# Longer estimated delays in the planner that lays down TensorE's order (RWKV scan of a hybrid attention layer)

## The chip, the cores and the metric

The kernel runs on one core of one Trainium2 chip. The time is the device time of one execution in microseconds (us); lower is better. Before the change three runs took 3445.99 us in the median (3438.13 to 3447.74).

## The reference

One layer for two groups of tokens, 512 "sample" and 128 "prompt" tokens of width 2048, in float32. An adaLN modulation is followed by one input projection. Its columns feed latent attention (8 heads) and a bidirectional RWKV-7 time mixing (16 heads of 64), whose state S is updated token by token in both directions. Then come one output projection, a post-norm, a SwiGLU feed-forward network and a second post-norm.

```python
def _wkv_scan(s0, r, decay, k, v, kk, a, reverse):
    def step(S, inp):
        r_t, w_t, k_t, v_t, kk_t, a_t = inp
        sa = jnp.einsum("bhvk,bhk->bhv", S, -kk_t)
        S = S * w_t[:, :, None, :] + sa[..., None] * (kk_t * a_t)[:, :, None, :] + v_t[..., None] * k_t[:, :, None, :]
        return S, jnp.einsum("bhvk,bhk->bhv", S, r_t)
...
        logw = -jax.nn.softplus(-(w0 + jnp.tanh(wd) @ w_up).astype(F32)) - 0.5
        decay = jnp.exp(-jnp.exp(logw))
        a = jax.nn.sigmoid(a0 + ad @ a_up)
```

## The kernel before

Features lie on the 128 partitions and the 640 tokens along the free axis, in two halves of 320. Every large product is made from a high and a low part of each operand (`whi`, `wlo` of a weight, `xh`, `xl` of an activation), so one 128-column weight tile against one 128-row activation tile is three pairs of matmuls, one for each half.

The program has three stages in time. **Stage 1** computes the input projection (job `main`), the modulation vectors (`first_mods`, `wmods`) and, as soon as their columns are there, the RWKV scan (job `rwkv`). **Stage 2** begins when `main` has ended: attention takes the place of the projection beside what is left of the scan. **Stage 3** is the output projection and the feed-forward network; its order is not touched by the edited tables.

The scan is done in chunks of 64 tokens instead of token by token. It runs over 8 pairs of heads, and for each pair over two halves j = 0, 1: 16 **units**, one after another, each dependent on the last. A unit is a chain of small products on TensorE with work on VectorE (DVE), ScalarE (ACT) and GpSimd (POOL) between them:

- `rwkv_load` (once a pair): load r, k, v from DRAM, square k, a product with a block matrix (`m<-cst,kk`), a power on POOL, a product that spreads the result (`m<-cst,rt`);
- `rwkv_decays`: the low-rank products for decay and gate, one group for each direction (`m<-xw,lw`, `m<-xa,lw`, `m<-xl,lw`); for every unit but the first they are laid down by a side job, beside the chain of the unit ahead;
- `rwkv_prep`: operands `nk` and `pr` on DVE, ACT and POOL; then `rwkv_grams`: Gram products in three batches (`m<-pr,nk`), each evacuated by two ACT copies (to `mab`, `mrb`) and a DVE product;
- `inverse`: a long piece on DVE that ends in the tile `tc`, then four rounds of products (`m<-tc,mab`, `m<-pm,uc`, `m<-t,mab`, `m<-u,pm`);
- `rwkv_chain`: five state updates, each of three products: `m<-sv,pr` (evacuated to `xs`), `m<-xs,uf` (evacuated to `zv` by one ACT copy and one DVE copy), `m<-zv,bk` (to the next state `sv`); `outputs` adds the products of the step before.
- `rwkv_post` (once a pair, in a side job beside the next pair's first unit): group norm and the gate product `m<-sg,gw`, then a store of `y` to DRAM.

TensorE (PE) executes its instructions in order, and this order is written out by a small planner at build time, not by the framework. Each job is a generator; after it has issued a group of matmuls it yields an estimated delay in us. The planner keeps one clock, `T.now`, which advances by an estimate of each matmul's length. At each step it takes, of the jobs whose delay is over, the one with the lowest rank: the scan first (0), its side jobs, the modulation (2), attention (3), the projection (4).

```python
        now = max(self.pe.now, min(j.ready for j in free))
        job = min((j for j in free if j.ready <= now), key=lambda j: j.rank)
...
            job.ready = w if isinstance(w, Job) else self.pe.now + w
```

So a delay says how much work of the other jobs stands in PE's queue between a product of the scan and the next product that depends on it. The projection and attention are the filler. The delays are in two tables, `HOPS[0]` for stage 1 and `HOPS[1]` for stage 2. The planner has no say at run time: where a delay is too short, PE reaches the dependent product early and waits there, with the filler queued behind it. The orders on DVE, ACT and POOL, and on the queue SP that issues the DMAs, are made by the framework's own scheduler; they follow from PE's order.

Of the kernel before, what the change touches and what calls it, by code (L numbers as in the profile page):

```python
# [46 lines left out]
for _n, _w in (("ident", 128), ("gmask", 128), ("lmask", 32), ("par", 2), ("blk", 128), ("cen", 128), ("blk2", 2), ("sel", 2),  # L47
# [12 lines left out]
TURN = 0.5  # L60
W_HOP = 2.4
M_HOP = 4.9
RANK_R = 0
RANK_S = 1
RANK_W = 2
# [1 line left out]
RANK_Q = 3  # L67
RANK_M = 4

HOPS = ({"load": 3.73, "pow": 3.84, "kk": 1.18, "dec": 0.92, "prep": 1.68, "vr": 2.17, "tv": 0.36, "bk": 0.36, "gram": 0.75,  # L70
         "inv": 12.0, "d32": 1.2, "d32b": 1.92, "d64": 1.44, "d64b": 1.44, "x": 0.48, "s": 0.72, "p": 0.72,
         "bon0": 0.92, "bon": 0.36, "cen0": 0.0, "cen": 0.36, "ysq": 0.28, "pow2": 3.84, "gup0": 0.0, "gup": 0.36,
         "wm": 5.98, "ev": 1.0, "sq": 3.77},
        {"load": 3.69, "pow": 2.76, "kk": 0.42, "dec": 0.36, "prep": 3.6, "vr": 1.2, "tv": 0.85, "bk": 0.54, "gram": 0.79,
         "inv": 14.0, "d32": 1.51, "d32b": 1.96, "d64": 1.3, "d64b": 1.44, "x": 0.61, "s": 0.72, "p": 0.72,
         "bon0": 0.94, "bon": 0.36, "cen0": 0.0, "cen": 0.51, "ysq": 0.71, "pow2": 3.84, "gup0": 0.0, "gup": 0.36,
         "rms": 2.33, "krs": 7.15, "rope": 0.6, "sc": 0.0, "turn": 0.0, "val": 0.0})
N_WS = 2
# [81 lines left out]
def step_kernel(ctx: ExitStack, tc: tile.TileContext, a: dict, o: dict, upto: int = 99, npairs: int = NPAIR, dbg=None):  # L160
    nc = tc.nc
    HOP = dict(HOPS[0])
    V, A, G, DMA = nc.vector, nc.scalar, nc.gpsimd, nc.sync
# [21 lines left out]
    def rtile(name, n, tag, bufs, dtype=F32):  # L185
        return rp.tile([P, n], dtype, tag=tag, name=nm(name), bufs=bufs)

    def slot(name, dtype=F32):
        return rtile(name, NT, "s", N_S, dtype)
# [7 lines left out]
    def half5(name):  # L197
        return rtile(name, 512, "h5", 4)
# [18 lines left out]
    def vcol(name, i=0, n=1):  # L217
        return vec[:, VEC[name][0] + i: VEC[name][0] + i + n]

    def con(name):  # L220
        return cst[:, CST[name][0]: CST[name][0] + CST[name][1]]
# [5 lines left out]
    def tt(eng, out, x, y, op):  # L227
        eng.tensor_tensor(out=out, in0=x, in1=y, op=op)  # L228
# [7 lines left out]
    def stt(out, x, s, y, op0, op1):  # L236
        V.scalar_tensor_tensor(out=out, in0=x, scalar=s, in1=y, op0=op0, op1=op1)

    def act(out, x, f, bias=0.0, scale=1.0):
        A.activation(out, x, f, bias=bias, scale=scale)  # L240
# [15 lines left out]
    def load_raw(src):  # L256
        raw = tile_("raw", 512, "raw", N_RAW)[:, :src.shape[-1]]
        DMA.dma_start(out=raw, in_=src)
        return raw
# [211 lines left out]
    def first_tiles():  # L471
        fs = (0, *range(2, 2 + N_PART), 1)
        ws = Weights(a["w_in"][f, k0 // 4][:, k0 % 4 * P: (k0 % 4 + nk) * P] for k0, nk in GROUPS for f in fs)
        for k0, nk in GROUPS:
            last = k0 + nk == KT
            while len(h1) < k0 + nk:
                yield 1.0
            yield M_HOP
            for f in fs:
# [56 lines left out]
    def rows(h):  # L536
        return slice(64 * h, 64 * h + 64)

    def ch(t):
        return t.rearrange("p (c t) -> p c t", t=C)  # L540
# [8 lines left out]
    def wide(name):  # L549

        return rtile(name, 2 * NT, "w", N_W).rearrange("p (c b t) -> p c b t", b=2, t=C)

    def h10(t):
        return t.rearrange("p (c t) -> p c t", t=32)
# [3 lines left out]
    for t in nd_bufs + u_bufs:  # L558
        G.memset(t, 0.0)

    def inverse(mab):

# [10 lines left out]
        x = half5("ix")  # L575
# [27 lines left out]
        tc_ = half5("tc")  # L603
        V.transpose(tc_[:, :HN], uc[:, :HN])
        u, t = h10(uc[:, :HN]), h10(tc_[:, :HN])
        yield HOP["inv"]
        blocks = [(e, b) for e in range(NCH) for b in range(4)]

        def d32(lhs, rhs):
# [14 lines left out]
        u, t = h10(u2[:, :HN]), h10(t2[:, :HN])  # L624
# [24 lines left out]
    def stat_cols(sq, rhs, n, bank=mps):  # L649

        ps = bank()
        for c in range(5):
            T.matmul(ps[:, c * n: c * n + n], sq[:, c * P: c * P + P], rhs, start=True, stop=True)
        return ps

    def spread(st, n, ps2=None):

        outs = []
        w_ = P // n
        for q, (c0, w) in enumerate(SPL):  # L660
            ps = mps() if ps2 is None else ps2[:, q, :]
            for j in range(w // P):
                c = c0 // P + j
                for e in range(n):
                    lhs = st[:, c * n + e: c * n + e + 1].broadcast_to([P, w_])
                    T.matmul(ps[w_ * e: w_ * e + w_, j * P: j * P + P], lhs, ident, start=True, stop=True)
            outs.append(ps)
        return outs

    def rpow(src, n, eps, scale, floor=False):  # L670
        st = small("st")
        if floor:
            ts(V, st[:, :n], src, eps, None, ALU.max)
        else:
            ts(V, st[:, :n], src, scale, eps)
        rt = small("rt")
        tt(G, rt[:, :n], st[:, :n], mhalf[:, :n], ALU.pow)
        return rt

    def nat(d, j):  # L680

        h = j if d == 0 else 1 - j
        return slice(h * HN, h * HN + HN)
# [5 lines left out]
    def rwkv_load(i):  # L689
        sh = {"carry": rtile("cy", 2 * C, "cy", 1)}  # L690
        raw = load_raw(a["lora"][i])

        lw = sh["lw"] = rtile("lw", 512, "lw", 1, F32R)
        A.copy(lw, raw)
        for r_, c_ in ((slice(64, 128), slice(0, 256)), (slice(0, 64), slice(256, 512))):
            tt(V, lw[r_, c_], raw[r_, c_], lw[r_, c_].bitcast(F32), ALU.subtract)
        for j, n in enumerate("rkv"):
            sh[n] = slot(n)
            DMA.dma_start(out=sh[n], in_=rkv_d[i][j])
        k = sh["k"]  # L700
        kk = sh["kk"] = slot("kk")
        act(kk, k, AF.Square, scale=vcol("kk", i))
        yield HOP["load"]
        ss = stat_cols(kk, con("blk2"), 2)
        rn = rpow(ss[:, :10], 10, 1e-24, 0, floor=True)
        yield HOP["pow"]
        for (c0, w), ps in zip(SPL, spread(rn, 2)):
            stt(kk[:, c0: c0 + w], k[:, c0: c0 + w], vcol("kk", i), ps[:, :w], ALU.mult, ALU.mult)
        sh["ks"] = slot("ks")
        yield HOP["kk"]  # L710
        return sh
# [43 lines left out]
    def rwkv_prep(i, j, sh, u):  # L755
        r, kk = sh["r"], sh["kk"]
        ld, ta, dd, nb = (u.pop(n) for n in ("ld", "ta", "dd", "nb"))
        nk = u["nk"] = wide("nk")
        pr = u["pr"] = [wide("pr") for _ in range(2)]
        dd5 = ch(dd)  # L760
        for h in range(2):
            rh = rows(h)
            stt(nk[rh, :, h, :], ch(nb)[rh], -0.5, ch(ld)[rh], ALU.mult, ALU.mult)
            tt(V, nk[rh, :, 1 - h, :], ch(ta)[rh], ch(ld)[rh], ALU.mult)
            for d in range(2):
                es = slice(5 * d, 5 * d + 5)
                kv_, rv_ = (ch(t[rh, nat(d, j)]) for t in (kk, r))
                if d == 1:
                    kv_, rv_ = kv_[:, ::-1, ::-1], rv_[:, ::-1, ::-1]
                tt(V, pr[h][rh, es, 0, 1:C], kv_[:, :, 1:C], dd5[rh, es, 0:C - 1], ALU.mult)  # L770
                A.copy(pr[h][rh, es, 0, 0:1], kv_[:, :, 0:1])
                tt(G, pr[h][rh, es, 1, :], rv_, dd5[rh, es, :], ALU.mult)
        yield HOP["prep"]

    def rwkv_turned(i, j, sh, u):

# [180 lines left out]
    def rwkv():  # L957
        def start(i):
            while done["pair"] <= i:
                yield 1.0  # L960
            sh = yield from rwkv_load(i)
            u = yield from rwkv_decays(i, 0, sh)
            return sh, u

        def beside_first(i, sh, last):
            if last:
                yield from rwkv_post(*last)
            return sh, (yield from rwkv_decays(i, 1, sh))

        def beside_second(i, sh):  # L970
            yield from rwkv_bonus(i, sh)
            if i + 1 < npairs:
                return (yield from start(i + 1))

        sh, u = yield from start(0)
        last = None
        for i in range(npairs):
            for j in range(2):
                yield from rwkv_prep(i, j, sh, u)
                yield from rwkv_grams(u)  # L980
                turned = jobs.spawn(rwkv_turned(i, j, sh, u), TURN)
                side = jobs.spawn(beside_second(i, sh) if j else beside_first(i, sh, last), RANK_S)
                u["u"] = yield from inverse(u["mab"])
                yield turned
                yield from rwkv_chain(i, j, sh, u)
                last = (i, sh)
                yield side
                if side.result:
                    sh, u = side.result
        yield from rwkv_post(*last)  # L990
# [7 lines left out]
    if upto >= 2:  # L998
        jobs.spawn(rwkv(), RANK_R)
    mg = jobs.spawn(main(), RANK_M)  # L1000
# [16 lines left out]

    HOP.update(HOPS[1])

# [646 lines left out]
    for n in range(2):  # L1666
        if n:
            ms[0].clear()
        for f in range(KT):
# [10 lines left out]
            for g in range(4):  # L1680
                wh, wl = qs.get()
                for k in range(4):
                    x = ms[n][4 * g + k]
# [119 lines left out]
    for w in range(N_PRE):  # L1803
        if w % 2 == 0:
            s, u1 = [fslot("s"), fslot("s")], fslot("u1")
# [10 lines left out]
    for j in range(NF2):  # L1816
        if j == NF2 - 1:
            loads.enter_context(tc.manual_schedule(engines={mybir.EngineType.SP}))
        s, u1 = begun.pop(0) if begun else ([fslot("s"), fslot("s")], None)
# [246 lines left out]
```

## Time and profile before

The profiled execution took 3448.44 us; its span, from the first to the last instruction, is 3446.7 us.

| | before |
|---|---|
| median of three runs | 3445.99 us |
| profiled execution, and its span | 3448.44 us, 3446.7 us |
| PE idle in the span | 3446.7 - 3244.2 = 202.5 us |
| DVE, ACT, POOL busy | 2500.1, 1449.1, 993.8 us |
| first matmul of the scan | at 178.0 us |
| stage 2 (first matmul `acc<-cst,rms_s`) | from 1186.7 us |
| last gate product of the scan | at 1309.0 us |
| stage 3 (first matmul `b<-mh,qh`) | from 1468.3 us |

In a row of the trace "PE L114 MATMUL m<-pr,nk" is a matmul on TensorE, issued by line 114 (the helper through which most matmuls pass), that writes the PSUM tile `m` and reads the tiles `pr` and `nk`. A number in brackets is the idle time of the engine just before that row, with the instruction that released it. PEclk is the clock that TensorE was granted, as a share of full speed.

### The profile page before, as it was taken

Reading aid. Unit: us, or ns where it says so; the run is one execution under the profiler, and the core shown is the slowest. Engines: PE = TensorE matmul, PEld = TensorE weight load, DVE = VectorE, ACT = ScalarE, POOL = GpSimd, SP = SyncE. Lnnn points to the kernel's source line nnn. Section 1 sums busy time; section 2 is a strip of 40 time slices with the busy share of each in tenths; the row PEclk is TensorE's granted clock in tenths of the full one; section 3 lists DMA queues with packets and bytes.
Section 4 is the critical chain, followed back from the end, with each engine's and each line's share of the span. In section 5 each row is a group of like instructions: output and inputs, shape, how many; then the busy total and the mean of one; then the engine's idle time right before and its main releaser. Section 6 shows DMA issues by size and latency. Waiting matters only on the chain.

```text
span 3446.7 us, 71091 instructions
## 1 busy us (share of the span) xinstructions
PE 3244.2 (94%) x27746; PEld 2979.0 (86%) x27746; DVE 2500.1 (73%) x4469; ACT 1449.1 (42%) x3028; POOL 993.8 (29%) x1034
## 2 busy tenths in 40 slices
PE   7879899999998889999979999999999999999998
PEld 4667677777887778899979999999999999999997
DVE  3456676676677764467698988888887778999677
ACT  1334444444454344455454444444444444333234
POOL 0012212222212221102174444444443332222124
PEclk9989999999999899999989999999999999999998
DMA  9735444543222201085534443444343358888643
GB/s 359 237 115 165 137 147 158 163 144 127 62 64 62 83 28 47 29 267 175 154 104 141 167 129 126 142 135 129 124 143 115 119 185 287 302 284 289 219 142 119
DMA packets 289344, 527.71 MB, mean 153 GB/s; under 512 B 30512, under 2 KB 76272, under 8 KB 289008
## 3 DMA queue, kind: packets, MB, share of 16 engines
q1 hardware_dynamic: 289008, 523.18, 46.4%
q8 instruction: 217, 3.56, 0.4%
q14 instruction: 119, 0.97, 0.1%
HBM read 428.99 MB, written 92.44 MB: 151 GB/s over the span
## 4 chain that ended last, share of the span: by engine, by line
PE 56%; DVE 4%; issue 2%; ACT 2%; DMA 1%; POOL 1%; SPq 0%; ACTq 0%; DVEq 0%; POOLq 0%
PE b L114 50%; PE acc L114 4%; PE m L114 1%; DVE z L228 1%; DVE ql L228 1%; POOL z L228 1%; PE x L114 1%; DMA z<-zd 0%; PE acc L118 0%; ACT z L240 0%; DVE smx L1168 0%; ACT P L1169 0%; DVE raw L228 0%; DMA raw<-in_w_out_dram 0%; DMA raw<-in_w_down_dram 0%
## 5 line engine op out<-in xcount | busy, mean ns | idle before, releaser
L228 DVE TENSOR_TENSOR ql<-raw,qh 128x512 fp32r<-128x512 f32 (+1 forms) x1064 | 886.4, 847 | 266.2 <-ACT qh L1306 251.3
L1306 ACT CAST qh<-raw 128x512 fp32r<-128x512 f32 (+1 forms) x1064 | 632.9, 609 | 828.3 <-PE b L114 630.5
L114 PE MATMUL b<-t,qh 128*128 128x320 f32 x2816 | 623.9, 311 | 8.6 <-ACT qh L1306 7.5
L228 POOL TENSOR_TENSOR raw<-raw,raw 128x512 f32<-128x512 f32 x240 | 352.9, 1471 | 804.1 <-DVE ql L228 584.5
L114 PE MATMUL b<-op,qh 128*128 128x320 f32 x2560 | 550.8, 310 | 0.8 <-ACT qh L1306 0.5
L114 PEld LDWEIGHTS b<-t,qh 128*128 128x128 f32 x2816 | 473.8, 189 | 9.9 <-ACT qh L1306 8.4
L114 PE MATMUL b<-p,qh 128*128 128x320 f32 x2112 | 468.2, 310 | 0.8 <-ACT qh L1306 0.8
L114 PE MATMUL b<-t,ql 128*128 128x320 f32 x1408 | 436.6, 311 | 4.6 <-DVE ql L228 4.6
L114 PEld LDWEIGHTS b<-op,qh 128*128 128x128 f32 x2560 | 424.2, 188 | 2.4 <-ACT qh L1306 1.0
L114 PE MATMUL b<-op,ql 128*128 128x320 f32 x1280 | 377.9, 310 | 7.6 <-DVE ql L228 7.5
L114 PEld LDWEIGHTS b<-p,qh 128*128 128x128 f32 x2112 | 355.5, 189 | 1.1 <-ACT qh L1306 1.0
L114 PE MATMUL b<-p,ql 128*128 128x320 f32 x1056 | 328.5, 311 | 6.5 <-DVE ql L228 6.4
L114 PE MATMUL acc<-xh,whi 128*128 128x320 f32 x1056 | 270.0, 338 | 1.9 <-ACT xh L271 1.9
L114 PEld LDWEIGHTS b<-t,ql 128*128 128x128 f32 x1408 | 265.5, 189 | 6.5 <-DVE ql L228 6.5
L114 PE MATMUL acc<-xl,whi 128*128 128x320 f32 x1056 | 265.1, 333 | 0.5 <-DVE xl L228 0.5
L114 PE MATMUL acc<-xh,wlo 128*128 128x320 f32 x1056 | 261.6, 330 | 0.0
L114 PEld LDWEIGHTS b<-op,ql 128*128 128x128 f32 x1280 | 235.9, 188 | 10.2 <-DVE ql L228 10.1
L114 PE MATMUL b<-mh,qh 128*128 128x320 f32 x1024 | 230.2, 314 | 7.3 <-ACT qh L1306 7.3
L114 PEld LDWEIGHTS b<-p,ql 128*128 128x128 f32 x1056 | 199.3, 189 | 9.1 <-DVE ql L228 9.1
L114 PEld LDWEIGHTS acc<-xh,whi 128*128 128x128 f32 x1056 | 180.9, 198 | 28.3 <-issue 13.1
L114 PEld LDWEIGHTS acc<-xl,whi 128*128 128x128 f32 x1056 | 181.2, 197 | 24.1 <-issue 14.0
L228 DVE TENSOR_TENSOR raw<-raw,raw 128x512 f32<-128x512 f32 x240 | 185.0, 778 | 11.1 <-POOL raw L228 9.2
(330 smaller groups left out, 5416.8 us busy)
## 6 DMA issues: line engine op xcount, KB each, us to landing
wm<-in_w_mod_dram SPq DMA_DIRECT2D x64, 1024.0 KB, 5.4
raw<-in_w_gate_dram SPq DMA_DIRECT2D x188, 256.0 KB, 2.7
raw<-in_w_up_dram SPq DMA_DIRECT2D x188, 256.0 KB, 2.8
op<-hd SPq DMA_DIRECT2D x136, 320.0 KB, 5.3
wm<-in_w_mod_dram SPq DMA_DIRECT2D x64, 512.0 KB, 7.7
raw<-in_w_out_dram SPq DMA_DIRECT2D x128, 256.0 KB, 3.0
raw<-in_w_down_dram SPq DMA_DIRECT2D x128, 256.0 KB, 5.5
raw<-in_w_in_dram SPq DMA_DIRECT2D x127, 256.0 KB, 2.7
```

The costliest lines, as they stand in the source:

```text
L114: self.eng.matmul(out, lhsT, rhs, start=start, stop=stop)
L228: eng.tensor_tensor(out=out, in0=x, in1=y, op=op)
L1306: A.copy(hi, x)
```

## The change

Numbers in the planner's tables are raised, for both stages: `gram` 0.75 and 0.79 to 1.35 (the code yields twice this after each of the three Gram batches), `dec` 0.92 and 0.36 to 1.25 and 1.0 (also yielded twice over, after each direction's low-rank products), `s` 0.72 to 0.85 (between `m<-xs,uf` and `m<-zv,bk`). In the first unit alone three waits get an addition: 8 us after the load of pair 0, 7 us before the first Gram batch, 6 us before the first product of the inverse. No instruction is added or removed on PE; the same matmuls stand there in both orders.

```diff
+FIRST = (8.0, 7.0, 6.0)
...
-HOPS = ({"load": 3.73, "pow": 3.84, "kk": 1.18, "dec": 0.92, "prep": 1.68, "vr": 2.17, "tv": 0.36, "bk": 0.36, "gram": 0.75,
-         "inv": 12.0, "d32": 1.2, "d32b": 1.92, "d64": 1.44, "d64b": 1.44, "x": 0.48, "s": 0.72, "p": 0.72,
+HOPS = ({"load": 3.73, "pow": 3.84, "kk": 1.18, "dec": 1.25, "prep": 1.68, "vr": 2.17, "tv": 0.36, "bk": 0.36, "gram": 1.35,
+         "inv": 12.0, "d32": 1.2, "d32b": 1.92, "d64": 1.44, "d64b": 1.44, "x": 0.48, "s": 0.85, "p": 0.72,
...
-        {"load": 3.69, "pow": 2.76, "kk": 0.42, "dec": 0.36, "prep": 3.6, "vr": 1.2, "tv": 0.85, "bk": 0.54, "gram": 0.79,
-         "inv": 14.0, "d32": 1.51, "d32b": 1.96, "d64": 1.3, "d64b": 1.44, "x": 0.61, "s": 0.72, "p": 0.72,
+        {"load": 3.69, "pow": 2.76, "kk": 0.42, "dec": 1.0, "prep": 3.6, "vr": 1.2, "tv": 0.85, "bk": 0.54, "gram": 1.35,
+         "inv": 14.0, "d32": 1.51, "d32b": 1.96, "d64": 1.3, "d64b": 1.44, "x": 0.61, "s": 0.85, "p": 0.72,
...
-    def inverse(mab):
+    def inverse(mab, more=0.0):
...
-        yield HOP["inv"]
+        yield HOP["inv"] + more
...
-        yield HOP["load"]
+        yield HOP["load"] + (FIRST[0] if i == 0 else 0.0)
...
-        yield HOP["prep"]
+        yield HOP["prep"] + (FIRST[1] if i + j == 0 else 0.0)
...
-                u["u"] = yield from inverse(u["mab"])
+                u["u"] = yield from inverse(u["mab"], FIRST[2] if i + j == 0 else 0.0)
```

Because each delay shifts all that the planner lays down behind it, PE's order differs from the scan's first product to the end of stage 2. Three places show how. One added line at the top of the file makes the matmuls' line 115 instead of 114; the numbers behind the names count tiles.

The first place is PE where the scan begins. `kk` is the squared k of pair 0, and the rows `acc` are pairs of the projection. Before:

```order
L114 MATMUL acc_1505<-xh_240,whi_1499 128x320 x2
L114 MATMUL acc_1505<-xl_241,whi_1499 128x320 x2
L114 MATMUL acc_1505<-xh_240,wlo_1500 128x320 x2
L114 MATMUL m_1518<-cst,kk_1455 128x2 x5
L114 MATMUL acc_1505<-xh_249,whi_1499 128x320 x2
L114 MATMUL acc_1505<-xl_250,whi_1499 128x320 x2
```

After:

```order
L115 MATMUL acc_1505<-xh_904,wlo_1537 128x320 x2
L115 MATMUL acc_1505<-xh_913,whi_1536 128x320 x2
L115 MATMUL acc_1505<-xl_914,whi_1536 128x320 x2
L115 MATMUL acc_1505<-xh_913,wlo_1537 128x320 x2
L115 MATMUL m_1600<-cst,kk_1455 128x2 x5
L115 MATMUL acc_1505<-xh_922,whi_1536 128x320 x2
```

The product moved 29 rows down, past 27 pairs of the projection, one group of the modulation (`x<-wm`) and its summing product (`x<-cst,ev`). In the same way 37 pairs and two modulation groups stand between the last low-rank product and the first Gram batch of this unit, where 11 pairs and one group stood.

The second place is PE between the first and the second Gram batch of the first unit; the first and last rows belong to the two batches. Before:

```order
L114 MATMUL m_1709<-pr_1669,nk_1667 128x128
L114 MATMUL acc_1505<-xh_1184,wlo_1618 128x320 x2
L114 MATMUL acc_1505<-xh_1193,whi_1617 128x320 x2
L114 MATMUL acc_1505<-xl_1194,whi_1617 128x320 x2
L114 MATMUL acc_1505<-xh_1193,wlo_1618 128x320 x2
L114 MATMUL acc_1505<-xh_1202,whi_1617 128x320 x2
L114 MATMUL acc_1505<-xl_1203,whi_1617 128x320 x2
L114 MATMUL m_1736<-pr_1668,nk_1667 128x128
```

After:

```order
L115 MATMUL m_1876<-pr_1778,nk_1776 128x128
L115 MATMUL acc_1905<-xh_240,whi_1843 128x320 x2
L115 MATMUL acc_1905<-xl_241,whi_1843 128x320 x2
L115 MATMUL acc_1905<-xh_240,wlo_1844 128x320 x2
L115 MATMUL acc_1905<-xh_249,whi_1843 128x320 x2
L115 MATMUL acc_1905<-xl_250,whi_1843 128x320 x2
L115 MATMUL acc_1905<-xh_249,wlo_1844 128x320 x2
L115 MATMUL x_1575<-wm_352_1837,cs 32x512 x4
L115 MATMUL acc_1905<-xh_422,whi_1843 128x320 x2
L115 MATMUL m_1932<-pr_1777,nk_1776 128x128
```

Six pairs of the projection stood between the batches, and now seven and a modulation group of four matmuls (`x<-wm`) stand there; in most other units it is eleven pairs. Between `m<-xs,uf` and `m<-zv,bk` the usual filler goes from three pairs to four.

The third place is PE's last rows of stage 2. `PT`, `P` and `pp` belong to the last attention head, `rt` and `gw` to the last pair's post-processing. Before:

```order
L118 MATMUL m_17044<-cst,pp_17006 128x128
L114 MATMUL x_17012<-PT_17018,vS_16584 128x128 x5
L118 MATMUL acc_17053<-cst,P_16994 128x128 x5
L114 MATMUL m_17061<-pp_17006,vS_16584 128x128
L114 MATMUL x_17012<-PT_17052,vS_16584 128x128 x5
L118 MATMUL acc_17070<-cst,P_17038 128x128 x5
L114 MATMUL x_17012<-PT_17069,vS_16584 128x128 x5
```

After:

```order
L115 MATMUL m_17015<-cst,rt_16964 64x128 x6
L115 MATMUL m_17022<-cst,rt_16964 64x128 x4
L115 MATMUL m_17031<-sg_16913,gw_16910 128x320
L119 MATMUL m_17040<-cst,pp_16983 128x128
L115 MATMUL x_16989<-PT_16995,vS_16095 128x128 x5
L115 MATMUL m_17048<-sg_16913,gw_16910 128x320
L119 MATMUL acc_17053<-cst,P_16971 128x128 x5
L115 MATMUL m_17061<-pp_16983,vS_16095 128x128
```

The scan's last product stood 559 rows ahead of the end of stage 2, and now it stands 5 rows ahead of it. Stage 2 begins 316 rows earlier. Before, the Gram batches of one unit (the last) stood in it; now those of four units do.

## The prediction

> **What bounds the kernel now.** I read the page first, then PE's waits, then PE's rows in order of time at the largest of them, then the stretches by stage.
>
> ```profile
> span 3446.7 us, 71091 instructions
> PE 3244.2 (94%) x27746; PEld 2979.0 (86%) x27746; DVE 2500.1 (73%) x4469; ACT 1449.1 (42%) x3028; POOL 993.8 (29%) x1034
> PE   7879899999998889999979999999999999999998
> PEclk9989999999999899999989999999999999999998
> PE 56%; DVE 4%; issue 2%; ACT 2%; DMA 1%; POOL 1%; SPq 0%; ACTq 0%; DVEq 0%; POOLq 0%
> ```
>
> PE is busy 94% of the span and leads the chain that ended last (56% against 4% for DVE). The same matmuls are issued before and after, so time can only come from PE's idle 3446.7 - 3244.2 = 202.5 us and from matmuls that run at a lower granted clock. The edit acts from the scan's start to the end of stage 2, slices 2 to 17. PE's waits on the scan's tiles, grouped over the whole span (engine, tile, releaser: us in total, times, longest):
>
> ```profile
> PE m L114 <- DVE y L228: 25.6, 18, 2.3
> PE m L114 <- DVE t L228: 9.6, 3, 4.0
> PE m L114 <- DVE tc L604: 9.0, 5, 7.3
> PE m L114 <- ACT kk L240: 9.0, 1, 9.0
> PE m L114 <- ACT mrb L819: 8.2, 7, 2.1
> PE m L114 <- DVE zv L899: 8.1, 12, 1.8
> PE m L114 <- DVE nk L228: 7.7, 1, 7.7
> PE m L114 <- POOL sv L850: 7.0, 7, 1.3
> PE m L114 <- DVE sv L237: 4.7, 4, 2.3
> PE m L114 <- ACT zv L898: 1.3, 2, 0.9
> ```
>
> Three waits are single and long: 9.0 on `kk`, 7.7 on `nk`, 7.3 of the 9.0 on `tc`. They stand one after another in the first unit:
>
> ```profile
> 168.50 0.46 PE L114 MATMUL acc<-xh,wlo 128*128 128x320 f32 x2
> 177.99 2.29 PE L114 MATMUL m<-cst,kk 128*128 128x2 f32 x10 [9.04 <-ACT kk L240]
> 180.14 0.88 PE L114 MATMUL acc<-xh,whi 128*128 128x320 f32 x2
> 180.82 0.73 PE L114 MATMUL acc<-xl,whi 128*128 128x320 f32 x2
> 181.35 0.73 PE L114 MATMUL acc<-xh,wlo 128*128 128x320 f32 x2
> ...
> 185.43 0.45 PE L114 MATMUL acc<-xl,whi 128*128 128x320 f32 x2
> 185.72 0.46 PE L114 MATMUL acc<-xh,wlo 128*128 128x320 f32 x2
> ...
> 206.87 2.90 PE L114 MATMUL m<-pr,nk 64*128 64x128 f32 x16 [7.74 <-DVE nk L228]
> ...
> 242.92 1.29 PE L114 MATMUL m<-tc,mab 32*32 32x32 f32 x80 [7.31 <-DVE tc L604]
> ```
>
> The reader is to see two things: PE stops with projection pairs ready behind the waiting row, and after the wait it is slow. Pairs start 0.53 us apart at 181 us and 0.29 us apart (185.72 - 185.43) once it has recovered. The stretches by stage (start:end, length, then busy us of PE, PEld, DVE, ACT and POOL, granted clock, DMA share, GB/s):
>
> ```profile
> 168.00:243.00 75.00, 48.86 (x347) 40.67 (x349) 44.13 (x80) 27.19 (x65) 11.55 (x19) 0.82 0.39 126
> 243.00:400.00 157.00, 146.32 (x1995) 115.07 (x1996) 101.15 (x228) 64.31 (x168) 36.23 (x63) 0.94 0.45 144
> 600.00:800.00 200.00, 182.61 (x2334) 142.50 (x2330) 137.75 (x302) 85.14 (x219) 51.98 (x83) 0.96 0.46 149
> 1186.00:1250.00 64.00, 49.81 (x426) 40.96 (x426) 46.73 (x99) 27.91 (x72) 12.13 (x20) 0.79 0.26 83
> 1250.00:1310.00 60.00, 55.11 (x712) 48.59 (x712) 29.70 (x79) 22.70 (x56) 13.03 (x21) 0.94 0.08 23
> 1310.00:1400.00 90.00, 85.59 (x614) 81.28 (x613) 41.20 (x79) 39.76 (x90) 15.56 (x20) 1.00 0.15 47
> 1400.00:1468.00 68.00, 59.11 (x431) 55.94 (x429) 26.63 (x59) 27.06 (x63) 11.01 (x16) 0.98 0.13 39
> ```
>
> The first row is the first unit, the second and third are scan beside projection, the fourth is attention's start, the fifth is scan beside attention, and the last two are attention alone.
>
> **The change, part by part.** *First unit.* Filler now stands where PE waited. Ahead of `kk` come 27 pairs at 0.29 us, 7.8 us, and a modulation group with its summing product, about 1 us each: 9.8 us against 9.04. Ahead of the first Gram batch the filler grows by 26 pairs and a modulation group, 8.5 us against 7.74. Ahead of `tc` it grows by about 8 us (6 from the addition, 1.2 from the third Gram delay, each pair 10% longer than the planner thinks) against 7.31. PE need not run dry, since DMA is used to 39% in this stretch and DVE for 44.13 of 75 us. But the filler's weight splits queue on ACT and DVE beside the scan's own work, so I leave 1.6 of the 24.1 us: **-22.5** (bounds -24.1, and -12 if each `kk`, `nk` and `tc` moves out by half its wait).
>
> *Clock of that stretch.* 48.86 us busy at a clock of 0.82 is 48.86 x 0.82 / 0.94 = 42.6 us at the next stretch's 0.94: **-6** (bounds 0, and -8 if each restart costs what `kk` did: 9 pairs at 0.24 us extra and 1 us in `kk` itself would be 3 us each, less for `tc`). [...]
>
> *Gram batches.* `mrb` is the last tile that frees a Gram batch's PSUM bank. All of its 8.2 us in 7 waits stand behind a Gram batch, at the next batch or at the first product after the third; the longest is this:
>
> ```profile
> 823.03 1.69 PE L114 MATMUL m<-pr,nk 64*128 64x128 f32 x14 [2.09 <-ACT mrb L819]
> ...
> 1007.61 1.87 PE L114 MATMUL m<-pr,nk 64*128 64x128 f32 x14 [2.31 <-DVE y L228]
> ...
> 1078.07 1.13 PE L114 MATMUL m<-pr,nk 64*128 64x128 f32 x14 [1.14 <-POOL sv L850]
> ...
> 1141.74 1.13 PE L114 MATMUL m<-pr,nk 64*128 64x128 f32 x14 [1.72 <-DVE y L228]
> ```
>
> Six pairs (1.8 us) stood there and eleven (3.2 us) stand now, 1.4 us more: everything goes but 0.7 of the longest and a little elsewhere, **-7** (bounds -8.2 and -4).
>
> *State updates.* `zv` costs 8.1 + 1.3 = 9.4 us in 14 waits. One more pair covers 0.29 us of each, at most 4.1 us, and some of the 80 gaps had four pairs already: **-3** (bounds -4.1 and 0).
>
> *Low-rank products.* The change pushes back the second direction and the side job's end. No wait on the second direction is in the list above; those at the first are `y` waits, which stay. The products lie beside a unit of some 67 us (half of 1141.74 - 1007.61), which hides 1.3 us more: **0** (bounds 0 and +1 a unit where that cover is gone, at three units +3).
>
> *Units that change stage.* The scan now reaches to the end of stage 2, so units 13 to 15 run beside attention. Stage 2's table waits 3.6 instead of 1.68 us before the first Gram batch, which covers most of the waits at 1007.61, 1078.07 and 1141.74 (2.31 + 1.14 + 1.72 = 5.2): **-4** (bounds -5.2 and 0).
>
> *What stage 2 charges.* The three units are 3 x 67 = 200 us of PE queue. Beside the projection (600 to 800) PE idles 17.4 of 200 us, 8.7%. Beside attention (1250 to 1310) it idles 4.9 of 60, 8.2%, and the clock is 0.94 instead of 0.96: 2% slower, so 10% against 8.7%, +3 us. Stage 2 starts with the scan one step earlier in its unit, where only attention's first short products are filler: +2. Attention alone idles 4.4 + 8.9 us, of which 5.6 is the seam to stage 3 (below); the scan's products could fill some. **+5** (bounds -5 and +14, the latter with one softmax wait for each moved unit, 3.34 us and its clock):
>
> ```profile
> 1252.35 0.76 PE L118 MATMUL acc<-cst,P 128*128 128x128 f32 x5 [3.34 <-POOL P L234]
> ...
> 1468.33 0.90 PE L114 MATMUL b<-mh,qh 128*128 128x320 f32 x2 [5.61 <-ACT qh L1306]
> ```
>
> *Queues.* On SP the store of the last `y` now stands right ahead of attention's last store, and pair 6's ahead of two loads of attention weights. A late `y` would hold those up; its product stands 5 rows ahead of the end, over 3 us of attention, so the seam of 5.61 us should stay as it is. Stage 3 keeps its order on PE.
>
> Sum: -22.5 - 6 - 7 - 3 + 0 - 4 + 5 = -37.5 us. From the profiled execution, 3448.4 us, that is 3410.9; this execution lies 2.45 us above the median of the runs, 3445.99, so the forecast is **3408 us**.
>
> **The rivals.** *The first unit's waits only shrink.* `kk` is released by a chain of DRAM stores and loads, `nk` and `tc` by DVE and ACT, which must now also split the weights of the added filler. If two thirds of those 24.1 us stay as new waits and the clock does not recover, 8 us are left there, and 8 + 7 + 3 + 4 - 5 = 17: 3429 us. For it: DVE is already the releaser of most waits. Against: it is busy only 59% of that stretch.
>
> *Short waits carry a slow stretch too.* At 823.03 the 14 Gram matmuls took 1.69 us, against 1.13 at 1078.07. Counting a few slow pairs behind it, about 1.7 us go with such a wait. If all eight or so removed waits of about 1 us and more had it, 13 us would come on top: 3395 us. Against: at 1141.74, after 1.72 us of idle, the group took 1.13, so a short wait need not cost clock. [...]
>
> *Attention charges more (slower).* From 1186 to 1250, where attention had little ready and the scan's chain stood bare, PE idled 14.2 of 64 us (22%) at a clock of 0.79; against 0.96 that is 49.81 x (1 - 0.79 / 0.96) = 8.8 us more, 36% lost. If the three moved units ran so, they would lose 27% of 200 us more than beside the projection, 54 instead of 5: -37.5 + 49 = +11.5, 3457 us. It decides from the point where a moved unit costs 14 us more than it did in stage 1. At half this rate, +27 us instead of +5, the time is 3430; with the first unit's waits merely shrunk as well, 3451, no change.
>
> **How the numbers follow.** Forecast 0.54 (3396 to 3420), first rival 0.20 (3429), short waits with clock 0.14 (3395), attention at half the bare rate and little gained ahead of it 0.07 (3451), attention at the full bare rate 0.05 (3457). The range leaves out the last two and the low end of the second: 3390 to 3434. Such runs can tell 0.3%, about 10 us, from no change. Faster by more than that: 0.54 + 0.20 + 0.14 = 0.88; within it 0.07; slower 0.05.
>
> **What would show it.** In the new profile: no wait above 2 us on `kk`, `nk` or the first `tc`, and a granted clock near 0.94 from the scan's start on; `mrb` under 2 us in all; `zv` near 6; `y` near 21, with three units less in it; stage 3 beginning at about 1431 us with a seam of about 5.6 us; stage 3 as long as before. The forecast is wrong if the first unit's waits turn up under another releaser, if the scan beside attention shows a clock near 0.8 over its whole length, or if PE waits on `acc` for split weights.

## The result, and the profile after

The changed kernel takes 3415.1 us (median of four runs, 3407.0 to 3418.1) against 3446.9 us for the kernel before beside it: a ratio of 0.991, 95% interval 0.9895 to 0.993, or 31.8 us less. The forecast was 3408 us. One execution in all the experiments, of shift_only, took 7836.5 us, more than twice the others, and its ratio leaves it out. The profiled execution took 3418.1 us. The page of the changed kernel (span, busy time by engine, PE's granted clock in 40 slices):

```profile
span 3416.3 us, 71056 instructions
PE 3231.4 (95%) x27746; PEld 2973.9 (87%) x27746; DVE 2489.4 (73%) x4469; ACT 1447.3 (42%) x3028; POOL 994.2 (29%) x1034
PEclk9999998999998999999989999999999999999998
```

The span fell by 30.4 us: PE idles 184.9 us instead of 202.5 (-17.6) and is busy 3231.4 instead of 3244.2 us (-12.8) with the same 27746 matmuls. How much of the second figure is the clock is worked out under the clock term below. Four stretches of the kernel before: the first unit, the rest of stage 1, stage 2, stage 3 (length, then busy time of PE, PE's weight loads, DVE, ACT, POOL, then granted clock, DMA share, GB/s):

```profile
168.00:243.00 75.00, 48.86 (x347) 40.67 (x349) 44.13 (x80) 27.19 (x65) 11.55 (x19) 0.82 0.39 126
243.00:1186.70 943.70, 874.85 (x11396) 710.78 (x11396) 651.01 (x1443) 415.81 (x1067) 230.44 (x382) 0.96 0.37 118
1186.70:1468.33 281.63, 249.27 (x2175) 226.47 (x2171) 143.57 (x312) 117.45 (x277) 51.74 (x76) 0.93 0.15 47
1468.33:3446.70 1978.37, 1932.36 (x12952) 1909.77 (x12952) 1594.99 (x2499) 848.52 (x1543) 691.87 (x528) 0.98 0.53 174
```

And of the changed kernel:

```profile
168.00:243.00 75.00, 68.48 (x524) 57.45 (x526) 50.29 (x91) 33.20 (x77) 16.03 (x24) 1.00 0.58 187
243.00:1051.50 808.50, 758.45 (x9446) 622.28 (x9438) 515.25 (x1147) 337.04 (x861) 183.04 (x312) 0.95 0.40 129
1051.50:1437.98 386.48, 333.19 (x3940) 289.63 (x3934) 260.89 (x599) 186.73 (x469) 93.75 (x141) 0.93 0.13 40
1437.98:3416.30 1978.32, 1932.22 (x12952) 1912.04 (x12952) 1595.88 (x2499) 849.09 (x1543) 693.17 (x528) 0.98 0.53 174
```

Length less busy time is PE's idle time: 26.1 became 6.5 in the first stretch (-19.6), 68.9 became 50.1 in the rest of stage 1 (-18.8), and 32.4 became 53.3 in stage 2 (+20.9). Stage 3 is as long as it was and begins 30.3 us earlier. So the change won 38 us of idle time and gave 21 back in stage 2.

Some of PE's waits after the change (tile, releaser: us in total, times, longest):

```profile
PE m L115 <- DVE y L229: 22.1, 19, 2.7
PE x L115 <- DVE ev L360: 13.1, 10, 6.1
PE m L115 <- DVE zv L900: 6.5, 4, 4.1
PE m L115 <- ACT pm L635: 6.3, 6, 2.7
PE m L115 <- POOL sv L851: 6.0, 6, 1.2
PE acc L115 <- DVE wlo L229: 4.8, 2, 3.2
PE acc L119 <- DVE kl L229: 4.1, 2, 2.4
PE acc L115 <- DVE vS L1162: 3.5, 3, 2.0
PE acc L115 <- DVE ql L238: 3.1, 2, 1.9
PE m L115 <- DVE t L229: 1.6, 2, 0.8
PE m L115 <- ACT mrb L820: 0.4, 1, 0.4
```

`kk`, `nk` and `tc` have left the list, `mrb` fell from 8.2 to 0.4 and `t` from 9.6 to 1.6. New or longer are `ev` (5.5 before), `pm` (1.1), `wlo` (none), and three tiles of attention, `kl`, `vS` (none before) and `ql`. Before:

```profile
PE x L114 <- DVE ev L359: 5.5, 9, 0.9
PE acc L114 <- DVE kl L228: 0.7, 1, 0.7
PE acc L114 <- DVE ql L237: 0.3, 1, 0.3
```

Where stage 2 begins, PE's rows of the changed kernel show two waits of over 4 us on the scan:

```profile
1057.23 0.45 PE L115 MATMUL m<-xs,uf 64*64 64x64 f32 x8 [1.02 <-ACT xs L878]
1058.04 0.33 PE L115 MATMUL m<-zv,bk 128*64 128x64 f32 x2 [0.36 <-ACT zv L899]
1062.43 0.69 PE L115 MATMUL m<-zv,bk 128*64 128x64 f32 x6 [4.06 <-DVE zv L900]
1067.72 1.10 PE L115 MATMUL m<-sv,pr 128*64 128x64 f32 x7 [4.61 <-DVE sv L238]
```

The order of DVE over the same time shows why:

```profile
1057.10 1.64 DVE L238 SCALAR_TENSOR_TENSOR nk<-nb,ld 64x640 f32<-64x640 f32 x2
1058.77 0.89 DVE L229 TENSOR_TENSOR ta<-ta,k 128x320 f32<-128x320 f32 x2
1059.58 1.00 DVE L238 SCALAR_TENSOR_TENSOR araw<-araw,vec,acc 128x384 f32<-128x384 f32 x2
1060.50 1.55 DVE L229 TENSOR_TENSOR xl<-araw,xh 128x640 fp32r<-128x640 f32 x2
1062.08 0.29 DVE L900 COPY zv<-m 64x128 f32<-64x128 f32 x1
```

The copy to `zv` takes 0.29 us. The products that it reads (`m<-xs,uf`) end at 1057.68 us, and it begins at 1062.08, 4.4 us later. In between DVE ends `nk` and does `ta` for the scan, and `araw` and `xl` for attention (2.5 of the 4.4 us). PE waits 4.06 us. No idle time is shown on DVE in these rows. A delay in the planner's table is an estimate of this sum, not of the 0.29 us.

### The profile page after: what moved, and what is told of

Its sections match the earlier page's. It is cut to its first block, busy times and chain, and to the rows that moved or that the text cites. A ratio compares the mean times of both kernels' runs of the same rounds, so it can differ in the third digit from the quotient of the medians.

```text
span 3416.3 us, 71056 instructions
## 1 busy us (share of the span) xinstructions
PE 3231.4 (95%) x27746; PEld 2973.9 (87%) x27746; DVE 2489.4 (73%) x4469; ACT 1447.3 (42%) x3028; POOL 994.2 (29%) x1034
## 4 chain that ended last, share of the span: by engine, by line
PE 65%; DVE 8%; ACT 3%; issue 2%; DMA 2%; POOL 2%; SPq 0%; ACTq 0%; DVEq 0%; POOLq 0%
PE b L115 51%; PE acc L115 7%; PE m L115 5%; PE x L115 1%; DVE ql L229 1%; DVE pr L229 1%; POOL z L229 1%; DVE z L229 1%; DVE ip L229 1%; ACT z L241 0%; DMA z<-zd 0%; PE acc L119 0%; DMA k<-rkv 0%; DVE nk L238 0%; DVE wlo L229 0%
## 5 line engine op out<-in xcount | busy, mean ns | idle before, releaser
L115 PEld LDWEIGHTS acc<-xh,whi 128*128 128x128 f32 x1056 | 180.8, 197 | 33.5 <-issue 12.7
L229 DVE TENSOR_TENSOR wlo<-raw,whi 128x512 fp32r<-128x512 f32 (+1 forms) x161 | 110.3, 686 | 124.0 <-ACT whi L266 115.4
L115 PEld LDWEIGHTS acc<-xh,wlo 128*128 128x128 f32 x1056 | 180.6, 196 | 22.6 <-issue 9.2
```

Source lines behind the costliest of these rows:

```text
L115: self.eng.matmul(out, lhsT, rhs, start=start, stop=stop)
```

## The experiments

All times are medians, and each ratio is to executions of the kernel before beside them. Each piece of code shows what differs from the changed kernel, or, where it says "as before", what stands there in place of the change.

**The additions for the first unit alone (first_only)**

```diff
+FIRST = (8.0, 7.0, 6.0)
 "dec": 0.92 / 0.36, "gram": 0.75 / 0.79, "s": 0.72 / 0.72   (as before)
```

> The three additions for the first unit alone; the delays of the table as before. In PE's order one unit moves to stage 2 instead of three. Theory A (the first unit carries the gain): its idle time between 168 and 243 us falls by about 20 us and its clock rises to 1.0, worth some 9 us of busy time, and one moved unit charges about 5: -24 to -30 us, 3417 to 3423. Theory B (the clock comes back only with the waits of the later units): only the idle time goes, -12 to -18 us. The busy time of PE tells them apart: A has it about 9 us under that of before, B within 3 us.

Measured: 3421.2 us, ratio 0.9936 (0.9923 to 0.9948), 23.7 us less. Its first two stretches, and stage 2:

```profile
168.00:243.00 75.00, 70.80 (x510) 58.87 (x509) 49.41 (x90) 33.42 (x79) 15.73 (x24) 0.95 0.59 190
243.00:1133.60 890.60, 828.14 (x10778) 673.49 (x10777) 604.14 (x1358) 390.46 (x1004) 215.61 (x362) 0.96 0.37 119
1133.60:1445.66 312.06, 270.20 (x2624) 242.66 (x2622) 175.89 (x387) 137.66 (x327) 63.60 (x92) 0.93 0.14 43
```

The time is theory A's; 21.9 us of idle time left the first stretch and its clock rose to 0.95. But PE's busy time ahead of stage 3 (all its busy time less that of stage 3) is only 1 to 5 us below that of two executions of the kernel before (1306.9 against 1308.1 and 1311.9), not 9: on that point theory B was nearer. The records of the granted clock say otherwise. By the count explained under the clock term below, slow clock cost 56.0 us of busy time ahead of stage 3, against 61.8 and 66.4 before: 6 to 10 us less, which is theory A's size.

**The table alone (table_only)**

```diff
-FIRST = (8.0, 7.0, 6.0)
+FIRST = (0.0, 0.0, 0.0)
```

> The delays of the table as in the change; the three additions for the first unit at zero. Two units move to stage 2. By the steps of the prediction: Gram batches -7, state updates -3, changed stage two thirds of -4, stage 2 charges two thirds of +5: about -9 us. Theory A (stage 2 charges about 7 us of idle time for each unit that moves, as the changed kernel's windows suggest): -13 of shorter waits and +14 of stage 2: 0 us, within 5. Theory C (the longer delays also move the second unit's waits): slower by 3 to 8 us.

Measured: 3430.8 us, 0.9961 (0.9946 to 0.9976), 14.1 us less. Theories A and C fall; the prediction's own -9 lies in the interval. Two of the three long waits stay:

```profile
177.49 2.29 PE L115 MATMUL m<-cst,kk 128*128 128x2 f32 x10 [8.28 <-ACT kk L241]
206.32 2.90 PE L115 MATMUL m<-pr,nk 64*128 64x128 f32 x16 [6.71 <-DVE nk L229]
```

Both cost nearly what they did, while `tc` is gone (0.6 us in all) with no addition ahead of it. Part of that wait took another form: right ahead of the first product of the inverse, at 242.84 us, stand a wait of 1.30 us on `ev` and eight pairs that start 0.53 us apart. The two halves of the change come to 23.7 + 14.1 = 37.8 us apart and 31.8 together; with intervals of about 5 us on each, that difference can't be told from none.

**First unit and Gram batches (first_gram)**

```diff
-"dec": 1.25 / 1.0, "s": 0.85 / 0.85
+"dec": 0.92 / 0.36, "s": 0.72 / 0.72
```

> The additions for the first unit and the longer Gram delay; the delays for low-rank products and state updates as before. Three units move to stage 2, but about 80 rows of PE's order later than in the changed kernel. Theory A (low-rank and state delays add next to nothing to what PE waits for): within 4 us of the changed kernel, -28 to -36 us. Theory D (they push the scan deeper into attention, where it costs): 5 to 10 us faster than the changed kernel, -37 to -42 us. Theory E (the state delay carries real waits): zv stays at 9 us and the time is 3 to 6 us above the changed kernel's.

Measured: 3414.0 us, 0.9913 (0.9899 to 0.9928): the changed kernel's ratio to the last digit. Theory A holds. The low-rank and state delays together bring nothing that these runs can show.

**Stage 2's table undone (stage1_only)**

```diff
-"dec": 1.0, "gram": 1.35, "s": 0.85    (second table)
+"dec": 0.36, "gram": 0.79, "s": 0.72
```

> The additions for the first unit and the longer delays in stage 1's table; stage 2's table as before. The scan enters stage 2 at the same row of PE's order as in the changed kernel and ends some 90 rows earlier in it. Theory A (the charge of stage 2 comes from the units that stand there, whatever their delays): within 3 us of the changed kernel, -29 to -35 us. Theory D (it comes from stage 2's longer delays, which leave attention less filler at its own waits or starve the seam): 5 us or more faster than the changed kernel. Theory F (stage 2's longer delays hide Gram and low-rank waits there): 3 to 8 us slower than the changed kernel, with mrb above 3 us.

Measured: 3419.0 us, 0.993 (0.9914 to 0.9946). Theory D falls: it isn't faster. Between A and F it is open, since the interval overlaps the changed kernel's; but `mrb` stands at 4.9 us, 4.3 of them in stage 2, where the changed kernel shows none, and that is F's sign. Stage 2's idle time is 54.2 of 389.4 us, as in the changed kernel, so its sum doesn't hang on the second table's delays.

**The scan moved as a whole (shift_only)**

```diff
-FIRST = (8.0, 7.0, 6.0)
+FIRST = (75.0, 7.0, 6.0)
 "dec": 0.92 / 0.36, "gram": 0.75 / 0.79, "s": 0.72 / 0.72   (as before)
```

> The table as before, the first unit's additions with 75 us instead of 8 at its load: the scan as a whole starts later, and three units stand beside attention as in the changed kernel, where the first addition alone (first_only) moves one. Theory A (a moved unit costs about 4 to 6 us more beside attention than beside the projection): 8 to 12 us slower than first_only, 3429 to 3434 us, with about 52 us of PE idle time in stage 2. Theory B (moving units is free, and stage 2's idle time only stands in for stage 1's): within 3 us of first_only, 3418 to 3424 us.

Measured: 3435.1 us, 0.9977 (0.9964 to 0.9989): 14 us slower than first_only. Theory B falls. Its stretches:

```profile
168.00:243.00 75.00, 74.19 (x509) 64.64 (x508) 19.42 (x31) 19.70 (x38) 6.91 (x20) 1.00 0.71 228
243.00:1067.70 824.70, 755.52 (x9333) 616.53 (x9331) 545.81 (x1200) 349.65 (x895) 192.91 (x316) 0.95 0.38 123
1067.70:1460.63 392.93, 340.32 (x4060) 296.23 (x4058) 263.48 (x602) 187.94 (x471) 94.39 (x141) 0.92 0.12 39
```

Two more units stand in stage 2, and PE idles 52.6 us there instead of 41.9. The first unit now stands behind 243 us, so stage 1 is to be compared from 168 us on: it has two units less, and yet it idles 0.8 + 69.2 = 70.0 us against 4.2 + 62.5 = 66.7. So moving the scan in this way is not free, and the 10.7 us in stage 2 don't just replace waits of stage 1. Why stage 1 gave nothing back is not settled. PE waits 12.6 us on `mrb` in this kernel, 6.8 in first_only, so some of it may belong to this one order and not to the units that moved.

**Longer delays where waits were left (prep_longer, prep_gup_longer, prep_gup_ev_longer)**

```diff
-"prep": 1.68                        (first table)
+"prep": 3.0                         (prep_longer, and both below)
-"gup": 0.36 / 0.36
+"gup": 2.0 / 2.0                    (prep_gup_longer, and below)
-"ev": 1.0                           (first table)
+"ev": 4.0                           (prep_gup_ev_longer)
```

> The changed kernel with stage 1's delay ahead of the first Gram batch at 3.0 instead of 1.68. Theory A (the filler covers the waits of 1 to 2 us at a unit's first Gram batch): the waits on sv of POOL, 6.0 us, and about half of those on y of DVE, 22.1 us, go: -10 to -15 us against the changed kernel, 3400 to 3405 us. Theory B (what a longer delay saves, the next wait or stage 2 takes back): within 4 us of the changed kernel, 3411 to 3419 us.

> As prep_longer, and 2.0 instead of 0.36 behind each half of the gate product, ahead of the first low-rank product. Theory A: the y waits at the low-rank products, about 10 us, go too: 3392 to 3400 us. Theory B: within 4 us of the changed kernel, 3411 to 3419 us, with the idle time in other places.

> As prep_gup_longer, and 4.0 instead of 1.0 ahead of the modulation's summing product, where the changed kernel waits 13.1 us on ev, 6.1 of them at one place. Theory A: 8 to 12 us less than prep_gup_longer. Theory B: within 4 us of prep_gup_longer, since a unit more goes to stage 2, which charges for it.

Measured: 3404.4 us (0.9882, 0.9858 to 0.9906), 3390.6 us (0.9849, 0.9829 to 0.987) and 3390.0 us (0.9848, 0.9828 to 0.9868). Theory A for the first two (the second 1.4 us below its range), theory B for the third. In the waits of prep_gup_longer the `y` group has gone from 22.1 to 2.5 us, and another has grown:

```profile
PE m L115 <- DVE zv L900: 30.6, 15, 3.7
PE m L115 <- DVE y L229: 2.5, 6, 0.8
```

Part of what was hidden came back at the state updates, 6.5 to 30.6 us on `zv`. The gain came all the same, and not only from idle time: PE's busy time ahead of stage 3 fell from 1299.2 (changed kernel) to 1283.6 us.

**Both kernels once more (before_again, after_again)**

> The kernel before, unchanged, profiled once more: how far PE's busy and idle time and the beginning of stage 3 move between two executions of one program. If the clock of the first unit's stretch belongs to its waits, 168 to 243 us shows 0.78 to 0.86 again, and the busy time ahead of stage 3 lies within 5 us of 1311.9.

> The changed kernel, unchanged, profiled once more and timed in more rounds. If its lower busy time is no chance of one execution, the busy time ahead of stage 3 lies within 5 us of 1299.2 again, the clock of 168 to 243 us is 0.95 or more, and the time is 3411 to 3418 us.

The first stretch of the kernel before, then of the changed one, in these second executions:

```profile
168.00:243.00 75.00, 49.80 (x419) 41.49 (x419) 44.12 (x80) 27.15 (x65) 11.55 (x19) 0.80 0.38 125
```

```profile
168.00:243.00 75.00, 68.98 (x526) 58.24 (x524) 50.01 (x90) 34.40 (x80) 16.04 (x24) 1.00 0.59 190
```

Busy time ahead of stage 3 was 1308.1 and 1296.1 us, 12.0 apart against 12.7 in the first pair: the shorter busy time is no chance of one execution. The changed kernel took 3414.3 us, 0.9903 (0.9884 to 0.9922).

**The state delay raised for real (state_15, state_12)**

```diff
-"dec": 1.25 / 1.0, "s": 0.85 / 0.85
+"dec": 0.92 / 0.36, "s": 1.5 / 0.72     (state_12: "s": 1.2 / 0.72)
 "prep": 3.0 / 3.6, "gup": 2.0 / 2.0
```

> As prep_gup_longer, with stage 1's state delay at 1.5 instead of 0.85 and the low-rank and state delays that the change added to stage 2 undone. prep_gup_longer waits 30.6 us on zv, 23 of them in stage 1. A unit more moves to stage 2, and the scan ends 14 rows ahead of stage 3 instead of 55. Theory A (the real delay again, the charge of about 7 us idle for a unit that moves): -16 to -20 of zv, +7 for the unit: 8 to 14 us less than prep_gup_longer, 3377 to 3383 us. Theory G (the scan's end now stands bare at the end of stage 2, its filler used up): no better than prep_gup_longer or up to 15 us slower, with new waits in the last 60 us ahead of stage 3.

> As state_15 with 1.2 in place of 1.5, which moves about half as far. Theory A: 4 to 8 us less than prep_gup_longer, 3383 to 3387 us, zv at 12 to 18 us. Theory G: within 3 us of prep_gup_longer or slower, with new waits ahead of stage 3.

Measured: 3384.9 us (0.9831, 0.9812 to 0.9851) and 3390.2 us (0.984, 0.9822 to 0.9857). `zv` fell to 8.6 and 10.6 us, but neither time can be told from prep_gup_longer's: state_12's time is theory G's, and state_15's lies between the two theories. Stage 1 after 243 us, and stage 2, of prep_gup_longer:

```profile
243.00:1028.60 785.60, 747.78 (x9322) 614.74 (x9321) 516.13 (x1145) 335.17 (x857) 179.70 (x312) 0.96 0.41 133
1028.60:1406.94 378.34, 328.84 (x4061) 286.27 (x4059) 264.05 (x603) 187.97 (x471) 99.88 (x141) 0.95 0.13 41
```

And of state_15:

```profile
243.00:967.80 724.80, 704.16 (x8728) 580.62 (x8726) 475.57 (x1050) 311.80 (x792) 165.82 (x285) 0.98 0.43 141
967.80:1404.84 437.04, 372.90 (x4643) 319.75 (x4635) 303.04 (x695) 209.72 (x537) 114.86 (x166) 0.91 0.13 41
```

Idle time falls from 37.8 to 20.6 us in stage 1 and rises from 49.5 to 64.1 in stage 2, where the clock drops from 0.95 to 0.91. Of -17.2, 14.6 comes back. Part of it stands at the scan's last rows, as theory G had it:

```profile
1355.72 0.88 PE L115 MATMUL m<-tc,mab 32*32 32x32 f32 x80 [3.68 <-DVE tc L605]
1393.00 2.40 PE L115 MATMUL m<-cst,rt 128*64 128x128 f32 x20 [2.38 <-POOL rt L229]
1404.84 0.63 PE L115 MATMUL b<-mh,qh 128*128 128x320 f32 x1 [7.10 <-ACT qh L1307]
```

state_15 has the lowest time of the study. Beside the changed kernel on the same chip it takes 29.4 us less (3384.9 against 3414.3, intervals apart), and 1.7% less than the kernel before.

The kernels side by side, in us: the number of units whose inverse stands in stage 2, PE's idle time, its busy time ahead of stage 3, and where stage 3 begins. In shift_only the idle time from 243 us holds the first unit too.

| kernel | units | idle, 243 us to stage 2 | idle, stage 2 | busy ahead of stage 3 | stage 3 begins |
|---|---|---|---|---|---|
| before | 1 | 68.9 | 32.4 | 1311.9 | 1468.3 |
| before_again | 1 | 69.5 | 32.9 | 1308.1 | 1465.4 |
| first_only | 2 | 62.5 | 41.9 | 1306.9 | 1445.7 |
| table_only | 3 | 51.8 | 46.9 | 1306.2 | 1450.8 |
| first_gram | 4 | 51.6 | 52.8 | 1301.7 | 1440.1 |
| after | 4 | 50.1 | 53.3 | 1299.2 | 1438.0 |
| after_again | 4 | 55.2 | 51.2 | 1296.1 | 1438.1 |
| stage1_only | 4 | 51.6 | 54.2 | 1293.5 | 1435.5 |
| shift_only | 4 | 69.2 | 52.6 | 1309.9 | 1460.6 |
| prep_longer | 4 | 44.7 | 50.7 | 1298.6 | 1429.6 |
| prep_gup_longer | 4 | 37.8 | 49.5 | 1283.6 | 1406.9 |
| prep_gup_ev_longer | 5 | 36.8 | 47.8 | 1289.4 | 1411.8 |
| state_12 | 5 | 37.4 | 52.7 | 1290.4 | 1411.9 |
| state_15 | 5 | 20.6 | 64.1 | 1288.3 | 1404.8 |

## Why the prediction was right, and where its sizes were off

The prediction had the sign, most of the places and a range that holds the time. It forecast 37.5 us off the profiled execution; 30.3 came. By its own steps:

**First unit, -22.5: right in kind, 2.9 us short.** All three waits left the list, and 19.6 us of idle time left that stretch (19.2 in the second pair). For the weight splits 1.6 us were kept back; they turned out as `wlo`, 4.8 us in all in each of the two executions of the changed kernel. Waits on `acc` for split weights were one of the prediction's own signs of being wrong, and this sign came, though small. The rival in which the waits only shrink falls: none of the three is left, and first_only alone took 23.7 us.

**Clock, -6: right in place and size.** Of the four stretches shown above only this one was granted a higher clock: 0.82 became 1.00 (0.80 became 1.00 in the second pair). The rest of stage 1 went from 0.96 to 0.95 (to 0.97 in the second pair), and stage 2 stayed at 0.93 (0.94 became 0.93). The records of the granted clock show either full or half clock (1.0 or 0.5 in each of the 68 records of the kernel before and the 62 of the changed kernel). If each us of PE's busy time that lies at half clock is counted as 0.5 us lost, the loss in this stretch was 6.4 us (6.9 in the second pair) and is now none. From 243 us to stage 3 it was 52.6 (49.0) and is 53.7 (46.9), so nothing clear was won there. In all, ahead of stage 3, it fell from 66.4 to 60.2 us (61.8 to 53.0), by 6 to 9 us.

PE's busy time fell by 12.7 and 12.0 us there. The other 6.4 and 3.2 us of it are not in the records of the clock, and what they are stays open. Pairs of 0.46 us start 0.29 us apart (185.43 and 185.72 us in the kernel before), and busy time counts such an overlap once, so it may also move with the order: counted at full clock it lies anywhere from 1235.7 to 1250.9 us in the 14 profiles.

*Short waits carry a slow stretch too*, the rival of 0.14, shows in part in the runs. The Gram products of one kernel after another (busy us and mean ns, then the idle time ahead of them), in the order before, its second execution, first_only, the changed kernel, prep_gup_longer:

```profile
L114 PE MATMUL m<-pr,nk 64*128 64x128 f32 x640 | 64.1, 310 | 32.9 <-DVE y L228 10.7 <-DVE nk L228 7.7 <-POOL sv L850 7.0
L114 PE MATMUL m<-pr,nk 64*128 64x128 f32 x640 | 61.8, 301 | 34.2 <-DVE y L228 10.7 <-DVE nk L228 7.7 <-POOL sv L850 7.0
```

```profile
L115 PE MATMUL m<-pr,nk 64*128 64x128 f32 x640 | 66.4, 315 | 25.7 <-DVE y L229 10.6 <-ACT mrb L820 5.5 <-POOL sv L851 5.1
```

```profile
L115 PE MATMUL m<-pr,nk 64*128 64x128 f32 x640 | 55.4, 292 | 14.0 <-DVE y L229 7.5 <-POOL sv L851 6.0 <-ACT mrb L820 0.4
```

```profile
L115 PE MATMUL m<-pr,nk 64*128 64x128 f32 x640 | 53.7, 293 | 3.0 <-DVE y L229 1.5 <-ACT mrb L820 0.8 <-ACT qh L241 0.7
```

The same 640 matmuls take 64.1 and 61.8 us before and 55.4 and 55.7 after. In the four kernels with the old Gram delay they take 59.6 (shift_only) to 66.4 us, in the ten with the longer one 53.6 to 58.2. By the count above, half clock cost this group 6.5 and 3.9 us before, 1.4 of them in the first unit, and 1.0 and 0.6 after. At 1141.74 us in the kernel before, the Gram products behind a wait of 1.72 us took 1.13 us, against 1.69 us behind the wait of 2.09 us at 823.03; so a wait need not have this cost, and how much of it goes with each is not shown. What this group won other products lost, since the sum from 243 us to stage 3 did not fall; so the rival's 13 us did not come.

**Gram batches, -7: right.** `mrb` fell by 7.8 us (9.4 to 2.0 in the second pair). first_only, without the longer delay, still waits 6.8 us on `mrb`. Not foreseen: `t` of the inverse fell by 8.0 us too (it stands at 11.6 in first_only).

**State updates, -3: near in size, by luck.** `zv` on DVE and ACT fell from 9.4 to 6.9 us, and 4.1 of what is left is the one new wait where stage 2 begins. But `zv` on DVE stands at 4.7 us in first_only and 6.8 in first_gram, which both keep the old state delay. So the fall came without it. **Low-rank products, 0: right**, as first_gram shows for both delays together.

**Units that change stage, -4: near in size, cause not shown.** `y` and `sv` fell from 37.3 to 33.1 us, and ahead of the Gram products from 10.7 + 7.0 = 17.7 to 7.5 + 6.0 = 13.5. But shift_only moves the same three units and still waits 9.6 + 7.1 = 16.7 us there, so the move alone does not do it.

**What stage 2 charges, +5: the term that was mis-sized.** Idle time in stage 2 rose by 20.9 us (18.3 in the second pair). The +5 was meant net of what the three units would have waited in stage 1; at the 68.9 / 15 = 4.6 us a unit of the kernel before that is 13.8, which leaves 7. But shift_only, where only the scan's start differs from first_only, moved two units and paid 14 us, since stage 1 gave nothing back. So the charge of three units, if it grows with their number, lies between 7 and 21 us, and +5 is below both ends.

The step that failed is the price, at three places. The rate at which PE idles beside attention was read from 60 us with one unit in it, 4.9 of 60 us or 8.2%; in the changed kernel PE idles 26.9 of the 263 us from 1115 to 1378, 10.2%. The rate beside the projection, 8.7%, still held waits that the change itself takes out; in the changed kernel it is 50.1 of 808.5 us, 6.2%. And the first 63.5 us of stage 2 idle 19.3 us where the first 63.3 idled 13.8, +5.4 instead of the +2 that was put down.

Who waits there differs with the order. In the changed kernel it is mostly attention: `kl`, `ql`, `vS`, `kh`, `PT` and `P` come to 10.4 us of PE's waits before and to 25.6 after, 15 of the 20.9. In first_gram stage 2 idles as long, 52.8 us, with 10.3 us on these tiles and 21.0 on the scan's `xs`, `tc` and `rt`. So the sum comes again in another order, and its place does not. DVE, which releases `kl`, `ql` and `vS`, is busy 260.89 of 386.48 us (68%) in stage 2, and was busy 143.57 of 281.63 (51%). That a wait goes through DVE's queue is shown at the beginning of stage 2 (`zv` behind `araw` and `xl`); for `kl`, `ql` and `vS` it is only argued. Beside this, `ev` (+7.6) and `pm` (+5.2) are longer waits, most of them in stage 1, that no term had.

In sum, the terms of idle time promised 37.5 - 6 = 31.5 us and 17.6 came, 13.9 too few; PE's busy time was to fall by 6 through the clock and fell by 12.8, 6.8 more, and of that fall a quarter to a half is in no record of the clock. That the two errors cancelled in half is luck, and it left the forecast 7 us off. Of the slower rivals, attention at the full bare rate (3457) would have shown a clock near 0.79 over the scan beside attention; it was 0.93.

## What to carry to other kernels

Where an order is written out ahead of time, the estimate at a hand-over has to hold the queue of the engine that answers, not only its instruction: a 0.29 us copy cost PE 4 us behind other work. The long waits that were removed paid twice, in idle time and in the clock of the products behind them: with three waits of 7 to 9 us went 19 to 20 us of idle time and 6 to 7 us of slow clock. For the many short ones these runs show no such sum. But filler is a budget: every delay pushes the chain into the next stage, so price the displaced work there by what it does to that stage's own chain.

## What the runs showed of the hardware

Stage 3 runs the same order in all kernels. Its length lay within 1975 to 1980 us while PE's busy time in it lay anywhere from 1923.8 to 1934.7: slower matmuls there mostly took up PE's idle time. The records of the granted clock account for the spread: counted at full clock, as above, its busy time is 1906.4 to 1909.2 us in all 14 profiles. So a difference of 10 us in the whole kernel's busy time says little by itself; ahead of stage 3, the two executions of each kernel agreed within 4 us.
